# Alternate columns: a matmul that reads its moving operand from two halves in turn

## The chip, the cores and the metric

The kernel runs on one core of a Trainium2 chip. The time is device microseconds of one execution on that core; the kernel before takes 2062.57 us (median of three runs, 2061.97 to 2063.31). The core has TensorE (matmul), VectorE, ScalarE, GpSimd and SyncE; in the profile they are PE (and PEld for its loads of the stationary operand), DVE, ACT, POOL and SP. On-chip data stands in SBUF; TensorE writes its results to PSUM, from which VectorE and ScalarE read them ("evict" them).

## The reference

One inference step of a two-layer decoder trunk with 512 prompt tokens and 32 sample tokens (8 sequences of 4), in float32, model width 1024. Layer 0 mixes tokens with a gated MLP, layer 1 with attention over keys and values that layer 0's output produces once.

```python
for i in range(DEPTH):
    h = h + 0.5 * swiglu(rmsnorm(h, ffn1_norm[i]), ffn1_w1[i], ffn1_w3[i], ffn1_w2[i])
    xn = rmsnorm(h, mix_norm[i])
    if i < N_A:
        mix, v_rows = gmlp_mix(xn, gmlp_w_in[i], gmlp_v_norm[i], gmlp_w_s[i], gmlp_b_s[i], gmlp_w_out[i])
    else:
        q = rmsnorm((xn @ att_w_q[j]).reshape(bsz, L, N_HEADS, HEAD_DIM), q_norm[j])
        if past is None:
            o = fox_prompt(q, k, v, lf)
        else:
            o = fox_sample(q, k, v, lf, past[0], past[1], past[2])
        mix = o.reshape(bsz, L, D_ATT) @ att_w_o[j]
    h = h + mix
    h = h + 0.5 * swiglu(rmsnorm(h, ffn2_norm[i]), ffn2_w1[i], ffn2_w3[i], ffn2_w2[i])
    gate = jax.nn.sigmoid(rmsnorm(h, ple_norm[i]) @ ple_w_gate[i])
    h = h + gate * (pe[i] @ ple_w_proj[i])
    if i == N_A - 1:
        kv = shared_kv(h, kv_norm, w_kvf, b_f, k_norm)
```

`swiglu(x, w1, w3, w2)` is `(silu(x @ w1) * (x @ w3)) @ w2` with an inner width of 2816. Nearly all of the arithmetic lies in its four calls.

## The kernel before

The activations are kept transposed: 8 chunks of 128 features (partitions) by T = 544 token columns (512 of the prompt, 32 of the samples); HT = 272 is half of that. A float32 product is made of three: each operand is split into a high part, rounded to the type that the listing calls F32R, and a low part, and high·high, high·low and low·high are added up in PSUM. These are the **split products**. In a matmul the weights are the stationary operand (128 by 128), and the token columns are the moving one.

[...] `mm` (L229 on, matmuls at L241, L245 and L247) is the common form; `tile_mm` calls it with the next weights, and the caller evicts the result, always in one instruction on VectorE or ScalarE.

The first products of a feed-forward layer (`ffn_steps`) go by Strassen's scheme: `products` makes seven half-size products k = 1 to 7 in place of eight, each with 24 matmuls of 272 columns (L491), into the buffers A, B and C; `evict` copies or adds them together (L499 to L513). `second` makes the products by w2 through `mm`, and its `update` (L530) adds them to the residual stream. `ffn_slots` lays down in what order both kinds come; the four engines keep that order, since this part is scheduled by hand. Weights are loaded, split by ScalarE (L198) and VectorE (L199) and, for Strassen, added (L184) a few units ahead by `prepare`.

Other split products: the gated MLP, the gates, the keys and the queries by `tile_mm`; the last gate chunk by `cols_mm` (L675), which finishes one part of `COLS` before the other; the values by `v_group` (L829 to L831), where the weights are the moving operand, 256 columns wide; attention's output by `product` (L1268 to L1275). The products inside attention (L1107 to L1161, 256 to 512 columns) and the small transposes and sums are no part of the change.

Of the kernel before, what the change touches and what calls it, by code (L numbers as in the profile page):

```python
# [84 lines left out]

CUT = 256
COLS = ((0, CUT), (CUT, T))


def whole(p):  # L90

    return p[:].rearrange("p a b -> p (a b)")[:, 512 - CUT:512 - CUT + T]


class Builder:
# [133 lines left out]
    def mm(self, out, w, x, first, last, mid=None):  # L229

        nc = self.nc
        out = whole(out)
        n = len(w)
        pin, self.pins = self.pins > 0 and first, self.pins - first
        for k in range(n):
            (wh, wl), (xh, xl) = w[k], x[k]
            if mid is not None and k == n - 1:
                mid()
            s, e = first and k == 0, last and k == n - 1
            for a, b in COLS:  # L240
                i = nc.tensor.matmul(out[:, a:b], wh, xh[:, a:b], start=s, stop=False)  # L241
                if pin and k == 0:
                    self.tc.keep_in_program_order(i)
            for a, b in COLS:
                nc.tensor.matmul(out[:, a:b], wh, xl[:, a:b], start=False, stop=False)  # L245
            for a, b in COLS:
                nc.tensor.matmul(out[:, a:b], wl, xh[:, a:b], start=False, stop=e)  # L247

# [157 lines left out]
    def ffn(self, h, box, gcol, rstd, on_chunk, plain=1):  # L406

        nc, eng = self.nc, mybir.EngineType
        self.ahead = (2, 3, 6)
        first, xs, xf = [], self.pairs(box), box["f"]  # L410

        def more(n):
            if len(xf) < min(n, NKP):
                xf.append(self.forms(h, gcol, len(xf), xs))
        hid, todo = {}, ([], [])
        lead = plain == 1 and len(xf) < 3
        for f in range(2 * plain):
            g = self.big()
            for w in range(2):
                if lead:  # L420
                    more(len(xf) + 1)
                if rstd is None:
                    p, rstd = self.tile_rstd(xs, box["acc"])
                else:
                    p = self.tile_mm(xs)
                nc.scalar.copy(g[:, w], whole(p))
# [38 lines left out]
    def ffn_steps(self, h, xf, rstd, hid, todo, plain, on_chunk):  # L465
        nc = self.nc
        add = ALU.add
        tt = nc.vector.tensor_tensor
        q2 = lambda t: t.rearrange("p (w b) -> p w b", w=2)
        tail = len(PARTS) - 1  # L470
        after = []
        w_of, tiles = {}, {}

        def products(j, k, part):
# [11 lines left out]
            for kp in range(NKP):  # L486
                xh, xl = xf[kp][k]
                for n, (a, b) in enumerate(((hi, xh), (hi, xl), (lo, xh))):
                    for w in range(2):
                        c = slice(512 * w + P * kp, 512 * w + P * kp + P)  # L490
                        nc.tensor.matmul(dst[w], a[:, c], b, start=k in "152" and kp == 0 and n == 0,  # L491
                                         stop=kp == NKP - 1 and n == 2, skip_group_check=True)
            after.append(lambda: evict(j, k))

        def evict(j, k):
# [8 lines left out]
            if k == "2":  # L504
                for w in range(2):
                    tt(g[0][:, w, :HT], t["B"][w], t["r1"][:, w], add)
            elif k == "7":
                tt(g[1][:, :, HT:], t["A"], t["r5"], add)  # L508
            elif k == "3":
                tt(g[0][:, :, HT:], t["C"], t["r6"], add)  # L510
                todo[0].extend(self.gate(hid, rstd, j, 0, g[0]))
            else:
                nc.scalar.copy(g[1][:, :, :HT], t["A"])  # L513
                todo[1].extend(self.gate(hid, rstd, j, 1, g[1]))
                del tiles[j]

        def second(p, c, part):
# [11 lines left out]
            def update():  # L529
                nc.vector.scalar_tensor_tensor(h[c], whole(out), 0.5, h[c], ALU.mult, ALU.add)  # L530
                if p == tail:
# [38 lines left out]
    def gmlp(self, h, box, on_chunk):  # L570
# [17 lines left out]
        for c in range(NC_):  # L588
# [7 lines left out]
            def take(p=p, vc=vt[:, c % 2, :]):  # L596
                nc.vector.tensor_tensor(vc, whole(p), rstd, ALU.mult)
                self.ssq(sq, vc, first=not v)
# [5 lines left out]
        def u_tile(c):  # L604
# [3 lines left out]
            us[c] = us["t"][:, c % 2, :]  # L608
            nc.vector.tensor_tensor(us[c], whole(p), rstd, ALU.mult)

# [54 lines left out]
        for c in range(NC_):  # L665
            p = self.tile_mm(m)
            nc.vector.tensor_tensor(h[c], whole(p), h[c], ALU.add)
            on_chunk(c)

    def cols_mm(self, outs, w, x):  # L670

        for (a, b), out in zip(COLS, outs):
            for k, ((wh, wl), (xh, xl)) in enumerate(zip(w, x)):
                for n, (u, v) in enumerate(((wh, xh), (wh, xl), (wl, xh))):
                    i = self.nc.tensor.matmul(out[:, :b - a], u, v[:, a:b], start=k == 0 and n == 0,  # L675
                                              stop=k == len(w) - 1 and n == 2)
# [3 lines left out]
    def ple_last(self, h, gates, rstd, xs, wp, pp, y):  # L680
# [6 lines left out]
        for (u, v), out in zip(COLS, outs):  # L687
            tt(a[:, u:v], out[:, :v - u], rstd[:, u:v], ALU.mult)
            nc.scalar.activation(a[:, u:v], a[:, u:v], AF.Sigmoid)
        outs = [self.ps()[:, 0, :], self.ps()[:, 0, :]]  # L690
        self.cols_mm(outs, wp[2 * c:2 * c + 2], pp)
        for (u, v), out in zip(COLS, outs):
            tt(a[:, u:v], out[:, :v - u], a[:, u:v], ALU.mult)
            tt(h[c][:, u:v], h[c][:, u:v], a[:, u:v], ALU.add)
            nc.sync.dma_start(out=y[c][:, u:v], in_=h[c][:, u:v])

    def ple(self, h, box, layer, on_chunk):
# [11 lines left out]
        for c in range(NC_ + 2):  # L709
            if c < NC_:  # L710
# [5 lines left out]
                def gate(p1=p1):  # L716
                    a = self.tmp()
                    nc.vector.tensor_tensor(a, whole(p1), rstd, ALU.mult)
                    nc.scalar.activation(a, a, AF.Sigmoid)
# [5 lines left out]
            for n in (range(c - 2, c + 1) if last and c == NC_ - 2 else [c - 2] if c >= 2 else ()):  # L725
                p2 = self.ps()
                self.mm(p2, wp[2 * n:2 * n + 2], pp, True, True)
                a = gates[n]
                nc.vector.tensor_tensor(a, whole(p2), a, ALU.mult)
                nc.vector.tensor_tensor(h[n], h[n], a, ALU.add)  # L730
# [37 lines left out]
    def kv(self, h, box, ffn_gain):  # L768
# [4 lines left out]
        f = self.big()[:, 0, :]  # L773
        self.evac(lambda p=p: nc.vector.tensor_tensor(f, whole(p), rstd, ALU.mult))
        self.bg.append(self.forget(f))
# [11 lines left out]
        def k_tile(hh):  # L787
# [4 lines left out]
            def take(p=p, kc=box["k"][:, hh % 2, :]):  # L792
                box["last"] = nc.vector.tensor_tensor(kc, whole(p), rstd, ALU.mult)
                kraw.append(kc)
# [14 lines left out]
        def v_group(g, beside):  # L809
# [13 lines left out]
            for i in range(4):  # L823
# [3 lines left out]
                for k, (wh, wl) in enumerate(w):  # L827
                    xh, xl = xs[k]
                    nc.tensor.matmul(out, xh[:, t], wh, start=k == 0, stop=False)  # L829
                    nc.tensor.matmul(out, xh[:, t], wl, start=False, stop=False)  # L830
                    nc.tensor.matmul(out, xl[:, t], wh, start=False, stop=k == NC_ - 1)  # L831
                for f in beside[i]:
                    f()
            for i in range(4):
                nc.scalar.activation(vi[:, i], p[:, 256 * i:256 * i + 256].rearrange("p (h d) -> p h d", h=2), AF.Copy,
                                     scale=rc[:, i:i + 1])
# [196 lines left out]
    def queries(self, xs, acc):  # L1033
# [4 lines left out]
        def tile(h):  # L1038
# [7 lines left out]
            def take(p=p, qc=box["q"][:, h % 2, :]):  # L1046
                box["last"] = nc.vector.tensor_tensor(qc, whole(p), box["rstd"], ALU.mult)
                q[h], sqs[h] = qc, self.square(qc)
# [31 lines left out]
    def attention(self, xs, acc, h_out, on_chunk):  # L1080
# [181 lines left out]
        def product(out, hs, w, ks, late=False):  # L1262
            hi, lo = w
            pin, self.pins = self.pins > 0, 0
            for n, k in enumerate(ks):
                c = slice(P * n, P * n + P)
                s, e = n == 0, n == len(ks) - 1
                i = nc.tensor.matmul(out, hi[:, c], o[k][:, 0, hs], start=s, stop=False)  # L1268
                if pin and s:
                    self.tc.keep_in_program_order(i)  # L1270
                if not late:
                    nc.tensor.matmul(out, hi[:, c], o[k][:, 1, hs], start=False, stop=False)  # L1272
                nc.tensor.matmul(out, lo[:, c], o[k][:, 0, hs], start=False, stop=e and not late)  # L1273
            for n, k in enumerate(ks if late else ()):
                nc.tensor.matmul(out, hi[:, P * n:P * n + P], o[k][:, 1, hs], start=False, stop=n == len(ks) - 1)  # L1275

        def project_half(c, part):
# [8 lines left out]
            with self.tc.issue_after(behind.ins) if behind else nullcontext():  # L1286
                nc.vector.tensor_tensor(out, p[:, :, :HT], out, ALU.add)
            for a in range(2) if part == 1 else ():
                on_chunk(2 * c + a, slice(0, HT))

        def project(c):
# [4 lines left out]
            out = h_out[c][:, HT:]  # L1296
            nc.vector.tensor_tensor(out, p[:, 0, :HT], out, ALU.add)
            on_chunk(c, slice(HT, T))
# [230 lines left out]
```

## Time and profile before

| | before |
|---|---|
| median of three timed runs | 2062.57 us |
| profiled execution: span | 2060.8 us |
| instructions | 38,864 |
| HBM read, written | 218.95 MB, 16.49 MB |
| DMA, mean over the span | 115 GB/s |
| ScalarE, waiting for VectorE before L198 | 262.5 us |
| VectorE, waiting for TensorE before L530 | 106.4 us |
| ScalarE, waiting for TensorE before L499 | 141.3 us |

The profile was taken on one execution; it states its span, from the first to the last instruction, and no other time for that execution. Its page gives busy times and the chain of work that ended last. A row of a group reads: line, engine, operation, output<-input by the program's tile names, partitions x elements of one instruction, and the count; then busy time in us, the mean of one in ns, and the idle time of the engine just ahead of them with what ended it. A row of the timeline begins with its start and its duration in us; equal instructions in a row are merged and counted. The duration of a matmul covers its way through the pipeline, so neighbours overlap: what a matmul costs in a stream is the distance from one start to the next.

### The profile page before, as it was taken

How to read it: one execution, taken by the hardware profiler on the slowest of the kernel's cores; microseconds unless marked ns; L12 is line 12 of the kernel's file. 1: busy time of each engine (PE TensorE's matmuls, PEld its weight loads, DVE VectorE, ACT ScalarE, POOL GpSimd, SP SyncE). 2: the span in 40 equal slices, each digit the busy share in tenths (PEclk: the TensorE clock that was granted, in tenths of full speed). 3: DMA queues.
4: the chain of work that ended last, by engine and by line, in shares of the span. 5: the costliest groups of instructions: out<-in, count | busy, mean ns of one | idle time of the engine just before them, and what ended most of it. 6: DMA issues, size and time to landing. Idle time of an engine off the chain costs nothing.

```text
span 2060.8 us, 38864 instructions
## 1 busy us (share of the span) xinstructions
PE 2045.6 (99%) x16442; PEld 2013.9 (98%) x16442; DVE 1506.0 (73%) x1862; ACT 950.9 (46%) x1421; POOL 185.6 (9%) x222
## 2 busy tenths in 40 slices
PE   9999999999999999999999999999999999999999
PEld 8999999999999999999999999999987999999999
DVE  7877777556687778776688777776476888777774
ACT  7535344423554344454456343534364754344451
POOL 0000000410100000043060000001131200000020
PEclk9999999999999999999999999999999999999999
DMA  5233234312223232432374323324669232222421
GB/s 185 84 111 107 74 109 141 97 45 83 83 93 113 72 104 82 154 99 82 103 261 161 113 86 110 107 66 136 192 211 320 96 100 84 102 103 82 130 97 44
DMA packets 93823, 237.95 MB, mean 115 GB/s; under 512 B 9538, under 2 KB 27490, under 8 KB 93650
## 3 DMA queue, kind: packets, MB, share of 16 engines
q1 hardware_dynamic: 93506, 235.44, 34.3%
q8 instruction: 129, 2.11, 0.4%
q14 instruction: 44, 0.36, 0.0%
q10 hardware_dynamic: 144, 0.04, 0.0%
HBM read 218.95 MB, written 16.49 MB: 114 GB/s over the span
## 4 chain that ended last, share of the span: by engine, by line
PE 92%; DVE 3%; ACT 2%; issue 1%; DMA 1%; SPq 0%; POOL 0%; DVEq 0%; ACTq 0%; POOLq 0%
PE ps L491 33%; PE ps L241 16%; PE ps L247 16%; PE ps L245 15%; PE pb L491 5%; DVE big L199 1%; ACT big L198 1%; PE ps L1268 1%; PE ps L1273 1%; PE ps L1272 1%; DVE big L184 0%; PE ps L1223 0%; PE ps L829 0%; PE ps L830 0%; PE ps L831 0%
## 5 line engine op out<-in xcount | busy, mean ns | idle before, releaser
L491 PE MATMUL ps<-big,big 128*128 128x272 f32 x5616 | 727.6, 288 | 1.8 <-DVE big L508 1.3
L491 PEld LDWEIGHTS ps<-big,big 128*128 128x128 f32 x5616 | 714.2, 188 | 2.4 <-issue 1.6
L199 DVE TENSOR_TENSOR big<-big,big 128x1024 fp32r<-128x1024 f32 (+2 forms) x538 | 590.8, 1100 | 106.4 <-ACT big L198 106.0
L198 ACT CAST big<-big 128x1024 fp32r<-128x1024 f32 (+2 forms) x538 | 488.0, 932 | 267.8 <-DVE big L184 262.5
L241 PE MATMUL ps<-big,big 128*128 128x256 f32 (+1 forms) x2684 | 558.2, 289 | 1.2 <-ACT big L198 0.8
L247 PE MATMUL ps<-big,big 128*128 128x256 f32 x2684 | 554.0, 288 | 1.9 <-DVE big L199 1.9
L245 PE MATMUL ps<-big,big 128*128 128x256 f32 x2684 | 553.8, 287 | 0.1
L241 PEld LDWEIGHTS ps<-big,big 128*128 128x128 f32 x2684 | 429.8, 188 | 5.3 <-issue 1.7
L247 PEld LDWEIGHTS ps<-big,big 128*128 128x128 f32 x2684 | 429.3, 188 | 3.7 <-DVE big L199 3.2
L245 PEld LDWEIGHTS ps<-big,big 128*128 128x128 f32 x2684 | 432.3, 189 | 0.5 <-DVE big L298 0.5
L326 POOL TENSOR_TENSOR st<-st,tmp 128x544 f32<-128x544 f32 (+1 forms) x63 | 89.0, 1412 | 1587.0 <-ACT tmp L324 1586.8
L530 DVE SCALAR_TENSOR_TENSOR big<-ps,big 128x544 f32<-128x544 f32 x160 | 115.5, 722 | 106.6 <-PE ps L247 106.4
L184 DVE TENSOR_TENSOR big<-big,big 128x1024 f32<-128x1024 f32 x156 | 190.0, 1218 | 0.0
L499 ACT COPY tmp<-ps 128x544 f32<-128x544 f32 x117 | 71.9, 614 | 141.3 <-PE ps L491 141.3
L454 ACT ACTIVATE big<-big 128x544 f32<-128x544 f32 x88 | 58.0, 660 | 163.0 <-DVE big L451 161.8
L491 PE MATMUL pb<-big,big 128*128 128x272 f32 x936 | 124.0, 288 | 0.0
L451 DVE TENSOR_TENSOR big<-big,st 128x1088 f32<-128x1088 f32 x88 | 113.3, 1289 | 10.6 <-ACT big L513 8.9
L491 PEld LDWEIGHTS pb<-big,big 128*128 128x128 f32 x936 | 120.2, 188 | 0.0
L286 DVE TENSOR_TENSOR big<-big,big 128x544 fp32r<-128x544 f32 (+1 forms) x112 | 81.5, 734 | 36.7 <-ACT big L285 36.5
L297 ACT ACTIVATE big<-big,gains 128x544 fp32r<-128x544 f32 (+1 forms) x80 | 55.6, 704 | 105.9 <-DVE big L530 64.9
L298 DVE SCALAR_TENSOR_TENSOR big<-big,gains,big 128x544 fp32r<-128x544 f32 (+1 forms) x80 | 66.7, 843 | 25.2 <-ACT big L297 25.2
L285 ACT CAST big<-big 128x544 fp32r<-128x544 f32 (+1 forms) x112 | 71.3, 644 | 16.2 <-DVE big L457 8.9
(213 smaller groups left out, 1436.5 us busy)
## 6 DMA issues: line engine op xcount, KB each, us to landing
big<-in_w SPq DMA_DIRECT2D x156, 512.0 KB
big<-in_w2a SPq DMA_DIRECT2D x64, 512.0 KB
big<-in_w2b SPq DMA_DIRECT2D x32, 384.0 KB
big<-in_w13p SPq DMA_DIRECT2D x16, 512.0 KB
big<-in_win SPq DMA_DIRECT2D x16, 512.0 KB
big<-in_wg SPq DMA_DIRECT2D x16, 512.0 KB
big<-in_ck SPq DMA_DIRECT2D x16, 512.0 KB
big<-in_cv SPq DMA_DIRECT2D x16, 512.0 KB
```

The source lines that it names most:

```text
L184: self.nc.vector.tensor_tensor(t, a, b, ALU.add if op == "+" else ALU.subtract)
L198: self.nc.scalar.copy(hi, src)
L199: self.nc.vector.tensor_tensor(lo, src, hi.bitcast(F32), ALU.subtract)
L241: i = nc.tensor.matmul(out[:, a:b], wh, xh[:, a:b], start=s, stop=False)
L245: nc.tensor.matmul(out[:, a:b], wh, xl[:, a:b], start=False, stop=False)
L247: nc.tensor.matmul(out[:, a:b], wl, xh[:, a:b], start=False, stop=e)
L286: self.nc.vector.tensor_tensor(pair[:, 1, cols], src, pair[:, 0, cols].bitcast(F32), ALU.subtract)
L326: nc.gpsimd.tensor_tensor(acc[:, cols], acc[:, cols], sq, ALU.add)
L451: tt(g, g, rstd.unsqueeze(1).broadcast_to([P, 2, T]), ALU.mult)
L491: nc.tensor.matmul(dst[w], a[:, c], b, start=k in "152" and kp == 0 and n == 0, stop=kp == NKP - 1 and n == 2, skip_group_check=True)
L499: nc.scalar.copy(t["r" + k], t["C" if k == "5" else "A"])
L530: nc.vector.scalar_tensor_tensor(h[c], whole(out), 0.5, h[c], ALU.mult, ALU.add)
```

## The change

Five helpers rearrange the access patterns. `woven(x)` walks through a stretch of columns by taking one from its first half, one from its second, and so on; `turns(out)` gives the output the same shape without changing its order, so the results lie in PSUM in the order in which they were made. `unwoven` reads such a result with a step of two elements, first all columns of the first half and then all of the second; `halves` splits the other operands and the destination alike. Every matmul of the split products named above reads its moving operand through `woven`. `COLS` now cuts in the middle, at 272; in `mm` each of the two matmuls takes 136 columns of either half of the tile. In `products` the two streams are the halves of 272 columns, in `v_group` the halves of 256 weight columns, one head each.

```diff
-CUT = 256
-COLS = ((0, CUT), (CUT, T))
+COLS = ((0, HT), (HT, T))
+def woven(x):
+    return x.rearrange("p (a b) -> p b a", a=2)
+def turns(out):
+    return out.rearrange("p (b a) -> p b a", a=2)
+def unwoven(out):
+    return out.rearrange("p (b a) -> p a b", a=2)
+def halves(x):
+    return x.rearrange("p (a b) -> p a b", a=2)
+def span(p):
+    return p[:].rearrange("p a b -> p (a b)")[:, 512 - HT:512 - HT + T]
 def whole(p):
-    return p[:].rearrange("p a b -> p (a b)")[:, 512 - CUT:512 - CUT + T]
+    return unwoven(span(p))
...
     def mm(self, out, w, x, first, last, mid=None):
-        out = whole(out)
+        out = turns(span(out))
+        parts = [(out[:, a // 2:b // 2], slice(a // 2, b // 2)) for a, b in COLS]
...
-            (wh, wl), (xh, xl) = w[k], x[k]
+            (wh, wl), (xh, xl) = w[k], map(woven, x[k])
...
-            for a, b in COLS:
-                i = nc.tensor.matmul(out[:, a:b], wh, xh[:, a:b], start=s, stop=False)
+            for o, b in parts:
+                i = nc.tensor.matmul(o, wh, xh[:, b], start=s, stop=False)
...
-                        nc.tensor.matmul(dst[w], a[:, c], b, start=k in "152" and kp == 0 and n == 0,
+                        nc.tensor.matmul(turns(dst[w]), a[:, c], woven(b), start=k in "152" and kp == 0 and n == 0,
...
-                    tt(g[0][:, w, :HT], t["B"][w], t["r1"][:, w], add)
+                    tt(halves(g[0][:, w, :HT]), unwoven(t["B"][w]), unwoven(t["r1"][:, w]), add)
...
-                tt(g[1][:, :, HT:], t["A"], t["r5"], add)
+                tt(h4(g[1][:, :, HT:]), u4(t["A"]), u4(t["r5"]), add)
...
-                nc.vector.scalar_tensor_tensor(h[c], whole(out), 0.5, h[c], ALU.mult, ALU.add)
+                nc.vector.scalar_tensor_tensor(halves(h[c]), whole(out), 0.5, halves(h[c]), ALU.mult, ALU.add)
...
-                    nc.tensor.matmul(out, xh[:, t], wh, start=k == 0, stop=False)
+                    nc.tensor.matmul(turns(out), xh[:, t], woven(wh), start=k == 0, stop=False)
...
-                i = nc.tensor.matmul(out, hi[:, c], o[k][:, 0, hs], start=s, stop=False)
+                i = nc.tensor.matmul(turns(out), hi[:, c], woven(o[k][:, 0, hs]), start=s, stop=False)
```

The other evictions (the gated MLP, the gates, the keys, the queries, attention's output) are rewritten in the same way as the update of the feed-forward layer. No engine gets its instructions in another order. What differs in the rows is the cut, here on TensorE in the first product of the program (tile `ps_190`; `big_120` is the split input, `big_123` and `big_124` the parts of the weights). Before:

```order
L241 MATMUL ps_190<-big_120,big_123 128x256
L241 MATMUL ps_190<-big_120,big_123 128x288
L245 MATMUL ps_190<-big_120,big_123 128x256
L245 MATMUL ps_190<-big_120,big_123 128x288
L247 MATMUL ps_190<-big_120,big_124 128x256
L247 MATMUL ps_190<-big_120,big_124 128x288
```

and of the change, the same place and the six matmuls after it:

```order
L267 MATMUL ps_190<-big_120,big_123 128x272 x2
L271 MATMUL ps_190<-big_120,big_123 128x272 x2
L273 MATMUL ps_190<-big_120,big_124 128x272 x2
L267 MATMUL ps_190<-big_127,big_123 128x272 x2
L271 MATMUL ps_190<-big_127,big_123 128x272 x2
L273 MATMUL ps_190<-big_127,big_124 128x272 x2
```

The two matmuls of a pair now have the same width and stand merged in one row; nothing moved.

More of the change, by code (lines that the diff above doesn't have):

```diff
@@ L239, in mm @@
             s, e = first and k == 0, last and k == n - 1
-            for a, b in COLS:
-                i = nc.tensor.matmul(out[:, a:b], wh, xh[:, a:b], start=s, stop=False)
+            for o, b in parts:
+                i = nc.tensor.matmul(o, wh, xh[:, b], start=s, stop=False)
                 if pin and k == 0:
                     self.tc.keep_in_program_order(i)
[L244 to L247, printed above, removed]
+            for o, b in parts:
+                nc.tensor.matmul(o, wh, xl[:, b], start=False, stop=False)
+            for o, b in parts:
+                nc.tensor.matmul(o, wl, xh[:, b], start=False, stop=e)
     def tile_mm(self, xs, mid=None):
@@ L674, in cols_mm @@
                 for n, (u, v) in enumerate(((wh, xh), (wh, xl), (wl, xh))):
-                    i = self.nc.tensor.matmul(out[:, :b - a], u, v[:, a:b], start=k == 0 and n == 0,
+                    i = self.nc.tensor.matmul(turns(out[:, :b - a]), u, woven(v[:, a:b]), start=k == 0 and n == 0,
                                               stop=k == len(w) - 1 and n == 2)
@@ L1271, in product @@
                 if not late:
-                    nc.tensor.matmul(out, hi[:, c], o[k][:, 1, hs], start=False, stop=False)
-                nc.tensor.matmul(out, lo[:, c], o[k][:, 0, hs], start=False, stop=e and not late)
+                    nc.tensor.matmul(turns(out), hi[:, c], woven(o[k][:, 1, hs]), start=False, stop=False)
+                nc.tensor.matmul(turns(out), lo[:, c], woven(o[k][:, 0, hs]), start=False, stop=e and not late)
             for n, k in enumerate(ks if late else ()):
-                nc.tensor.matmul(out, hi[:, P * n:P * n + P], o[k][:, 1, hs], start=False, stop=n == len(ks) - 1)
+                nc.tensor.matmul(turns(out), hi[:, P * n:P * n + P], woven(o[k][:, 1, hs]), start=False,
+                                 stop=n == len(ks) - 1)
         def project_half(c, part):
@@ L1296, in project @@
             out = h_out[c][:, HT:]
-            nc.vector.tensor_tensor(out, p[:, 0, :HT], out, ALU.add)
+            nc.vector.tensor_tensor(halves(out), unwoven(p[:, 0, :HT]), halves(out), ALU.add)
             on_chunk(c, slice(HT, T))
```

37 lines of the change are left out of this document (20 added, 17 removed).

## The prediction

> **What bounds the kernel now.** I read the page first: busy time, clock, chain.
>
> ```profile
> span 2060.8 us, 38864 instructions
> ...
> PE 2045.6 (99%) x16442; PEld 2013.9 (98%) x16442; DVE 1506.0 (73%) x1862; ACT 950.9 (46%) x1421; POOL 185.6 (9%) x222
> ...
> PEclk9999999999999999999999999999999999999999
> ...
> PE 92%; DVE 3%; ACT 2%; issue 1%; DMA 1%; SPq 0%; POOL 0%; DVEq 0%; ACTq 0%; POOLq 0%
> PE ps L491 33%; PE ps L241 16%; PE ps L247 16%; PE ps L245 15%; PE pb L491 5%; DVE big L199 1%; ACT big L198 1%; PE ps L1268 1%; PE ps L1273 1%; PE ps L1272 1%; DVE big L184 0%; PE ps L1223 0%; PE ps L829 0%; PE ps L830 0%; PE ps L831 0%
> ```
>
> TensorE is the bound from end to end at full clock, and 85% of the chain are the matmuls of L491, L241, L245 and L247. A busy engine may still be slowed by something that feeds it, so the next question is how far apart two matmuls start. The timeline merges equal matmuls; a merged row of n lasts n−1 spacings plus one matmul of 288 ns.
>
> ```profile
> 643.36 6.18 PE L491 MATMUL ps<-big,big 128*128 128x272 f32 x48
> ...
> 652.37 9.23 PE L491 MATMUL ps<-big,big 128*128 128x272 f32 x72
> ...
> 664.46 0.41 PE L241 MATMUL ps<-big,big 128*128 128x256 f32 x2
> ...
> 667.20 0.41 PE L247 MATMUL ps<-big,big 128*128 128x256 f32 x2
> ```
>
> 272 columns: (6.18−0.29)/47 = 125.3 ns and (9.23−0.29)/71 = 125.9 ns; I use **125.6**. The last two rows are the first and the twelfth pair of one product (256 and 288 columns in each pair): (667.20−664.46)/11 = **249 ns** a pair.
>
> What would the array alone need? The trace has a stretch in which the clock was granted by half:
>
> ```profile
> 9.68 0.66 PE L247 MATMUL ps<-big,big 128*128 128x256 f32 x2
> 10.14 0.66 PE L241 MATMUL ps<-big,big 128*128 128x256 f32 x2
> 10.59 0.66 PE L245 MATMUL ps<-big,big 128*128 128x256 f32 x2
> 11.04 0.66 PE L247 MATMUL ps<-big,big 128*128 128x256 f32 x2
> ```
> ```profile
> 8.00:11.40 3.40, 3.02 (x12) 2.69 (x13) 3.18 (x5) 2.98 (x5) 0.00 (x0) 0.56 0.94 367
> ...
> 700.00:704.00 4.00, 4.00 (x35) 4.00 (x34) 3.06 (x5) 3.08 (x4) 0.00 (x0) 1.00 0.50 135
> ```
>
> (In the last two rows the third figure from the end is the granted clock, the last one GB/s.) At the low clock (0.56 over that window, whose end is already faster) a pair takes (11.04−9.68)/3 = 453 ns, 0.833 ns a column. Twice the clock should give 0.417 ns a column, 227 ns a pair and 113 ns for 272 columns. The full clock gives 249 and 125.6: **12 ns of each matmul are not array time**. Wider matmuls, which this change doesn't touch, tell how that splits:
>
> ```profile
> 1514.44 0.40 PE L1107 MATMUL ps<-big,big 128*128 128x512 f32 x1
> ...
> 1515.37 0.27 PE L1115 MATMUL ps<-neg,identr 128*128 128x256 f32 x1
> ```
> ```profile
> 1538.53 0.28 PE L1107 MATMUL ps<-big,big 128*128 128x256 f32 x1
> ...
> 1539.00 0.28 PE L1115 MATMUL ps<-neg,identr 128*128 128x256 f32 x1
> ...
> 1539.94 0.39 PE L1107 MATMUL ps<-big,big 128*128 128x512 f32 x1
> ...
> 1540.86 0.28 PE L1115 MATMUL ps<-neg,identr 128*128 128x256 f32 x1
> ```
>
> Between each row and the next shown stand four spacings: 232 and 230 ns at 512 columns, 117.5 ns at 256. The slope is (230 to 232−117.5)/256 = 0.44 to 0.45 ns a column, 0.023 to 0.033 over the array's 0.417. Of the 12 ns, **6 to 9 grow with the columns**; the rest is fixed. So at full clock something that hands columns over, not the array, sets the pace, by 6 to 8%. The change alters just the order in which columns are fetched.
>
> **The change part by part.** No instruction is added, removed or reordered on any engine; only the columns' order, the cut and the access patterns differ. How many matmuls it touches:
>
> ```profile
> L491 PE MATMUL ps<-big,big 128*128 128x272 f32 x5616 | 727.6, 288 | 1.8 <-DVE big L508 1.3
> ...
> L241 PE MATMUL ps<-big,big 128*128 128x256 f32 (+1 forms) x2684 | 558.2, 289 | 1.2 <-ACT big L198 0.8
> L247 PE MATMUL ps<-big,big 128*128 128x256 f32 x2684 | 554.0, 288 | 1.9 <-DVE big L199 1.9
> L245 PE MATMUL ps<-big,big 128*128 128x256 f32 x2684 | 553.8, 287 | 0.1
> ...
> L491 PE MATMUL pb<-big,big 128*128 128x272 f32 x936 | 124.0, 288 | 0.0
> ```
> ```profile
> L1268 PE MATMUL ps<-big,big 128*128 128x272 f32 x128 | 37.2, 292 | 0.3 <-ACT big L198 0.3
> L1273 PE MATMUL ps<-big,big 128*128 128x272 f32 x128 | 36.8, 289 | 0.5 <-DVE big L199 0.5
> L829 PE MATMUL ps<-big,big 128*128 128x256 f32 x128 | 36.5, 285 | 0.0
> L830 PE MATMUL ps<-big,big 128*128 128x256 f32 x128 | 36.2, 283 | 0.0
> L831 PE MATMUL ps<-big,big 128*128 128x256 f32 x128 | 36.1, 282 | 0.0
> L1272 PE MATMUL ps<-big,big 128*128 128x272 f32 x120 | 34.5, 288 | 0.0
> ```
>
> 5616+936+3·2684+2·128+3·128+120 = 15,364 of 16,442, all of them on the path.
>
> *Fetching alternately.* No row shows a matmul that reads so, so I bound it. Best: all 12 ns go, 15,364 × 12 = 184 us. Worst: two neighbouring columns never come from one place, and each costs what a column costs at the half clock, 0.833 ns: 272 × 0.833 + 3 = 230 ns, +104 ns each, +1,600 us. The ends are far apart. The nearest rows are the 256 and 512 column ones: they show a stall that grows with the run of neighbouring columns. If it belongs to moving on along such a run, two runs read in turn give each twice the time for that step, and the stall hides. I take 7 of the 6 to 9 ns: **−108 us**. This is a choice, not a measurement; the rivals take the other ends.
>
> [...] No run here shows a strided matmul yet.
>
> *The cut, 256/288 to 272/272* (4,026 pairs of L241 to L247): 2 × 125.6 − 249 = +2 ns a pair, **+8 us**. Bounds: nothing to +10, as the two 272 rows differ by 0.6 ns.
>
> *Evictions with a stride.*
>
> ```profile
> L530 DVE SCALAR_TENSOR_TENSOR big<-ps,big 128x544 f32<-128x544 f32 x160 | 115.5, 722 | 106.6 <-PE ps L247 106.4
> ...
> L506 DVE TENSOR_TENSOR big<-pb,tmp 128x272 f32<-128x272 f32 x78 | 30.6, 433 | 8.6 <-PE pb L491 8.6
> L508 DVE TENSOR_TENSOR big<-ps,tmp 128x544 f32<-128x544 f32 x39 | 28.2, 724 | 48.3 <-PE ps L491 48.3
> L510 DVE TENSOR_TENSOR big<-ps,tmp 128x544 f32<-128x544 f32 x39 | 28.2, 724 | 30.7 <-PE ps L491 30.5
> ```
> ```profile
> 650.00:1000.00 350.00, 350.00 (x2810) 349.97 (x2809) 259.87 (x292) 157.26 (x216) 39.69 (x32) 1.00 0.29 96
> ...
> 1520.00:1650.00 130.00, 126.63 (x1152) 112.24 (x1152) 97.04 (x184) 80.91 (x184) 34.18 (x69) 1.00 0.68 225
> ```
>
> A column more costs VectorE (724−433)/272 = 1.07 ns. Nothing shows a PSUM read with a stride, so the bounds are 0 and that again: +0.58 us for 544 columns, 238 × 0.58 + 78 × 0.29 = 161 us of VectorE work. VectorE is 260 of 350 us busy in a feed-forward layer (74%; the first row's sixth figure is its busy time), and the groups above were waiting for TensorE already. With 161 us more, VectorE would be at 1506 + 161 = 1667 of 2061 us, 81%. What is spare hides it, so I take 0; the cover is gone where TensorE waits for the eviction itself, and then each costs up to its 0.58 us.
>
> *What comes late next.* In attention (1520 to 1650) TensorE already waits 3.4 of 130 us; some of that stage's share of the gain is lost to those waits, +7 us. Weights arrive at 96 GB/s in the feed-forward window where another moved 367, so 5% more is covered. The load of the stationary operand, 98% busy on the page, must be asked too, since each matmul has one:
>
> ```profile
> 470.20 0.60 PE L618 MATMUL ps<-consts,big 128*128 128x128 f32 x4
> ```
>
> Four matmuls of 128 columns follow each other by (0.60−0.27)/3 = 110 ns (0.27 for one, next to the 0.28 of the 256-column rows), where their 128 columns need 53. So loads allow 110 ns, below the 118.6 that I forecast; they are no bound yet, and they would be one only past the best end.
>
> **Sum:** 2060.8 − 108 + 8 + 7 = 1967.8 us of span. The profile gives no time beyond the span; the timed median, 2062.57, lies 1.8 above it, so **about 1969 us**.
>
> [...]
>
> **Rivals.**
> 1. *Each column pays its own fetch* (slower). Place: all 15,364 matmuls. [...] Price: from zero to 0.417 ns a column; at the full price 2062.6+1600 ≈ 3660 us. It decides as soon as it costs more than the stall saves, 7 ns a matmul or 0.026 ns a column. A partial price of 0.07 ns a column would give about 2350. [...]
> 2. *The stall doesn't care about order*: it is a pause every so many columns, or the fixed part. Then only the cut remains: 2063 to 2071 us. For it: the same slope in 256 and 512 wide reads with different operands.
> 3. *Strided PSUM reads cost double and are not hidden* at the 160 updates of L530: if TensorE waits for every one, 160 × 0.58 = 93 us. Without a gain on TensorE 2062.6 + 8 + 93 = 2164; with it 2062. For it: L530 is the largest group that reads PSUM. Against: its 106.4 us of idle time before, spent waiting for TensorE.
>
> **How the numbers follow.** Forecast 0.48 (1900 to 2055 by its own bounds). Rival 1: 0.30, of it 0.12 with a partial price (2067 to 2350), 0.18 beyond. Rival 2: 0.16, of it 0.10 within 0.2% (about what a measurement here can tell from no change). Rival 3: 0.06, of it 0.02 still faster. So faster 0.50, same 0.10, slower 0.40. Leaving out rival 1's expensive part (0.18) and 0.02 of tails, the range is 1900 to 2350; the likeliest case alone would be 1900 to 2055.
>
> **What would show it.** Right: runs of 24 to 72 matmuls of the Strassen line at 117 to 120 ns instead of 125.6, TensorE still at 98% or more, VectorE's evictions still at 722 ns. Rival 1: spacings well over 126, up to 230 ns, with every other engine waiting. Rival 2: 125.6 unchanged. Rival 3: L530's mean near 1,300 ns instead of 722 and TensorE waiting for it. The forecast fails first at its choice of 7 ns, since no row of this trace prices an alternate read.

## The result

The changed kernel takes 1936.35 us (median of four runs, 1936.06 to 1937.12) against 2062.27 us for the kernel before: a ratio of 0.939, 95% interval 0.9377 to 0.9404. 126 us are gone. The page of the profiled execution after:

```profile
span 1934.7 us, 38865 instructions
...
PE 1908.8 (99%) x16442; PEld 1873.7 (97%) x16442; DVE 1502.2 (78%) x1862; ACT 946.9 (49%) x1421; POOL 185.3 (10%) x222
...
PE 85%; DVE 7%; ACT 4%; issue 2%; DMA 2%; SPq 1%; POOL 0%; DVEq 0%; ACTq 0%
```

The same number of matmuls in 136.8 us less of busy time (2045.6 to 1908.8), and all other engines as busy as before, to within 4 us. TensorE is still 99% busy: that figure said nothing of the room that was there. The time in which TensorE isn't busy (span less its busy time) went from 15.2 (2060.8 − 2045.6) to 25.9 us (1934.7 − 1908.8); 136.8 − 10.7 = 126.1 us is the gain in span.

The timeline of TensorE after (start, duration, instruction, count) has the spacings:

```profile
603.33 5.72 PE L519 MATMUL ps<-big,big 128*128 128x272 f32 x48
608.89 0.40 PE L267 MATMUL ps<-big,big 128*128 128x272 f32 x2
...
611.44 0.40 PE L273 MATMUL ps<-big,big 128*128 128x272 f32 x2
611.67 8.50 PE L519 MATMUL ps<-big,big 128*128 128x272 f32 x72
```

272 columns: (5.72−0.28)/47 and (8.50−0.28)/71 give **115.8 ns** both times (0.28 us is the last matmul alone), where the rows before gave 125.3 and 125.9. A pair of the common form takes (611.44−608.89)/11 = 231.8 ns instead of 249. The evictions, in the groups by shape (the last row is ScalarE's largest; before, at L499, its mean was 614 ns):

```profile
L558 DVE SCALAR_TENSOR_TENSOR big<-ps,big 128x544 f32<-128x544 f32 x160 | 115.4, 721 | 75.8 <-PE ps L273 75.8
...
L534 DVE TENSOR_TENSOR big<-pb,tmp 128x272 f32<-128x272 f32 x78 | 30.7, 437 | 1.8
L536 DVE TENSOR_TENSOR big<-ps,tmp 128x544 f32<-128x544 f32 x39 | 28.2, 724 | 35.7 <-PE ps L519 35.7
L538 DVE TENSOR_TENSOR big<-ps,tmp 128x544 f32<-128x544 f32 x39 | 28.1, 722 | 25.9 <-PE ps L519 25.9
```
```profile
L527 ACT COPY tmp<-ps 128x544 f32<-128x544 f32 x117 | 71.5, 611 | 89.7 <-PE ps L519 89.7
```

721, 437, 724 and 722 ns against 722, 433, 724 and 724 on VectorE, 611 against 614 on ScalarE: reading PSUM in steps of two float32 costs neither engine anything that these rows can show, beyond the 4 ns of the 272-wide row. What did shrink is their idle time, since TensorE comes round sooner: 75.8 us before L558 where it was 106.6.

### The profile page after: what moved, and what is told of

Read it like the earlier page. It is cut to its first block, busy times and chain, and to the rows that moved or that the text cites. A ratio compares the mean times of both kernels' runs of the same rounds, so it can differ in the third digit from the quotient of the medians.

```text
span 1934.7 us, 38865 instructions
## 1 busy us (share of the span) xinstructions
PE 1908.8 (99%) x16442; PEld 1873.7 (97%) x16442; DVE 1502.2 (78%) x1862; ACT 946.9 (49%) x1421; POOL 185.3 (10%) x222
## 4 chain that ended last, share of the span: by engine, by line
PE 85%; DVE 7%; ACT 4%; issue 2%; DMA 2%; SPq 1%; POOL 0%; DVEq 0%; ACTq 0%
PE ps L519 30%; PE ps L267 14%; PE ps L273 14%; PE ps L271 14%; PE pb L519 5%; DVE big L224 2%; ACT big L223 1%; DVE big L209 1%; DVE big L312 1%; DMA tmp<-rows 1%; ACT big L311 1%; DVE big L477 0%; PE ps L1251 0%; PE ps L657 0%; PE ps L857 0%
## 5 line engine op out<-in xcount | busy, mean ns | idle before, releaser
L519 PE MATMUL ps<-big,big 128*128 128x272 f32 x5616 | 674.1, 279 | 5.9 <-DVE big L536 3.4
L519 PEld LDWEIGHTS ps<-big,big 128*128 128x128 f32 x5616 | 660.8, 189 | 7.1 <-issue 4.0
L224 DVE TENSOR_TENSOR big<-big,big 128x1024 fp32r<-128x1024 f32 (+2 forms) x538 | 593.7, 1106 | 88.7 <-ACT big L223 87.2
L223 ACT CAST big<-big 128x1024 fp32r<-128x1024 f32 (+2 forms) x538 | 485.1, 928 | 271.1 <-DVE big L209 267.1
L267 PE MATMUL ps<-big,big 128*128 128x272 f32 x2684 | 533.5, 280 | 5.6 <-ACT big L223 4.0
L273 PE MATMUL ps<-big,big 128*128 128x272 f32 x2684 | 531.5, 279 | 3.6 <-DVE big L224 3.5
L271 PE MATMUL ps<-big,big 128*128 128x272 f32 x2684 | 530.6, 279 | 0.3 <-DVE big L324 0.3
L267 PEld LDWEIGHTS ps<-big,big 128*128 128x128 f32 x2684 | 409.6, 189 | 11.5 <-ACT big L223 7.3
L273 PEld LDWEIGHTS ps<-big,big 128*128 128x128 f32 x2684 | 409.2, 189 | 6.1 <-DVE big L224 5.7
L271 PEld LDWEIGHTS ps<-big,big 128*128 128x128 f32 x2684 | 409.4, 189 | 0.8 <-DVE big L324 0.7
L558 DVE SCALAR_TENSOR_TENSOR big<-ps,big 128x544 f32<-128x544 f32 x160 | 115.4, 721 | 75.8 <-PE ps L273 75.8
L519 PE MATMUL pb<-big,big 128*128 128x272 f32 x936 | 114.8, 279 | 0.0
L519 PEld LDWEIGHTS pb<-big,big 128*128 128x128 f32 x936 | 111.3, 189 | 0.0
```

The costliest lines, as they stand in the source:

```text
L223: self.nc.scalar.copy(hi, src)
L224: self.nc.vector.tensor_tensor(lo, src, hi.bitcast(F32), ALU.subtract)
L267: i = nc.tensor.matmul(o, wh, xh[:, b], start=s, stop=False)
L271: nc.tensor.matmul(o, wh, xl[:, b], start=False, stop=False)
L273: nc.tensor.matmul(o, wl, xh[:, b], start=False, stop=e)
L519: nc.tensor.matmul(turns(dst[w]), a[:, c], woven(b), start=k in "152" and kp == 0 and n == 0, stop=kp == NKP - 1 and n == 2, skip_group_ch ...
```

## The experiments

Three sorts: streams of matmuls put ahead of the changed kernel's work, which price one way of reading each; the change done or undone in part; and one version that goes further. A stream is 24 matmuls with one operand each; its spacing is (duration of its row − the last matmul's duration) / 23, and the text gives the mean over its start times. The kernel's own work follows unchanged, so the total times of those runs mean nothing here.

### Streams, first set (bench)

```diff
+        x, w, hx = self.flat(1024, F32R), self.flat(1024, F32R), self.flat(1024, mybir.dt.bfloat16)
...
+        weave = lambda n, a=2: x[:, :n].rearrange("p (a b) -> p b a", a=a)
+        group = lambda n, c: x[:, :n].rearrange("p (a b c) -> p b a c", a=2, c=c)
+        local = lambda n, b: x[:, :n].rearrange("p (g a b) -> p g b a", a=2, b=b)
+        step = lambda n, a: x[:, :n].rearrange("p (b a) -> p a b", a=a)
...
+        for _ in R: mm(o(272), W, x[:, :272], start=True, stop=True)
+        for _ in R: mm(f3(272, 2), W, weave(272), start=True, stop=True)
...
```

Here `mm` is the matmul, `R` the 24 repetitions, `W` 128 columns of weights, and `o` and `f3` shape the output. `step` reads every a-th column, then goes back for the next set, until all are read. `local` takes turns between neighbouring runs of b columns, `group` takes c columns at a time from each half. Each set was profiled in one execution. Where a row stands in two sets, the two agree within 1.4 ns: contiguous 272 columns took 125.3 and 126.7 ns, woven ones 115.9 and 116.0, two columns at a time 175.4 and 174.6.

> The changed kernel with 31 streams of 24 matmuls each put ahead of its work, on one float32 operand (F32R) of random numbers, 128 by 128 weights; a stream's spacing is read from its row of the timeline. Theory A (the stall belongs to moving on along one run of neighbouring columns, and two runs read in turn hide it): contiguous 256, 272, 384, 512 columns at about 117, 125, 176, 232 ns; woven halves at N x 0.417 + 2.5 = 109 to 112, 116, 162.5, 216 ns; four and eight streams as two, 116; pairs and fours of neighbours read in turn lie between 116 and 125; two streams only 2 or 4 columns apart still share one run and stay at 122 to 125, those 16 or 64 columns apart reach 109 to 112 at 256 columns. [...] Theory C (the stall is a conflict with the load of the next weights): loading 32 instead of 128 weight columns takes it away from contiguous reading too, 116 ns; and a single column read 272 times over still has it. Theory D (it is the width of the element): two-byte operands have no stall when contiguous, 116 ns at 272 and 216 ns at 512 columns, and the weave changes nothing for them.

The rows of the timeline, in order: contiguous and woven at 272, 256, 384 and 512 columns (L1356 to L1363); then four and eight streams (L1364, L1365); further down two streams 2 and 4 columns apart (L1370, L1371), steps of 2 and 4 (L1375, L1376), 32 columns of weights, contiguous (L1382), and two-byte columns, contiguous (L1384, 272 wide) and woven (L1386, 512 wide).

```profile
14.60 3.17 PE L1356 MATMUL pb<-big,big 128*128 128x272 f32 x24
17.61 2.94 PE L1357 MATMUL pb<-big,big 128*128 128x272 f32 x24
20.39 3.03 PE L1358 MATMUL pb<-big,big 128*128 128x256 f32 x24
23.25 2.84 PE L1359 MATMUL pb<-big,big 128*128 128x256 f32 x24
25.93 4.36 PE L1360 MATMUL pb<-big,big 128*128 128x384 f32 x24
30.14 4.06 PE L1361 MATMUL pb<-big,big 128*128 128x384 f32 x24
34.03 5.65 PE L1362 MATMUL pb<-big,big 128*128 128x512 f32 x24
39.52 5.34 PE L1363 MATMUL pb<-big,big 128*128 128x512 f32 x24
44.70 3.65 PE L1364 MATMUL pb<-big,big 128*128 128x272 f32 x24
48.19 5.77 PE L1365 MATMUL pb<-big,big 128*128 128x272 f32 x24
...
67.12 3.18 PE L1370 MATMUL pb<-big,big 128*128 128x272 f32 x24
70.14 2.94 PE L1371 MATMUL pb<-big,big 128*128 128x272 f32 x24
...
81.06 6.08 PE L1375 MATMUL pb<-big,big 128*128 128x272 f32 x24
86.96 6.10 PE L1376 MATMUL pb<-big,big 128*128 128x272 f32 x24
...
112.68 3.20 PE L1382 MATMUL pb<-big,big 128*32 128x272 f32 x24
...
118.50 2.95 PE L1384 MATMUL pb<-big 128*128 128x272 bf16 x24
...
126.47 11.79 PE L1386 MATMUL pb<-big 128*128 128x512 bf16 x24
```

| read | ns | read | ns |
|---|---|---|---|
| contiguous 256, 272, 384, 512 | 119.4, 125.3, 175.1, 228.8 | woven halves, same widths | 111.7, 115.9, 162.4, 215.8 |
| two streams 2, 4, 8 columns apart (272) | 125.9, 115.8, 115.8 | two streams 16, 64 apart (256) | 111.6, 111.7 |
| four, eight streams (272) | 145.2, 232.7 | 2, 4, 8 columns at a time (272) | 175.4, 131.0, 130.0 |
| step 2, 4, 8 (272); step 16 (256) | 246.1, 246.6, 233.4; 219.8 | one column for ever (272) | 119.9 |
| contiguous, starting 1 or 2 columns later (272) | 125.3, 126.5 | 16 columns at a time (256) | 120.0 |
| weights of 32 columns: contiguous, woven (272) | 126.5, 115.7 | two-byte: contiguous 272, 512; woven 512 | 116.3, 215.9; 484.3 |

The 2.5 ns that theory A adds to N x 0.417 is what the changed kernel's 115.8 ns leave over 272 columns at the half-clock estimate of 0.417 (113.3). Theory C falls: with 32 columns of weights to load in place of 128 the stall stays (126.5), and a woven read with the same weights has none (115.7). D holds for its first half, two-byte columns don't stall when contiguous (116.3 ns at 272, 215.9 at 512); weaving them costs more than double (484 against 216), which nobody expected. A is right about two halves (115.9), but not about runs: 4 columns apart, inside one run, is as good as half a tile apart (115.8), while 2 apart is worth nothing (125.9), and four streams are worse than one (145.2 against 125.3). Four float32 are 16 bytes, and columns 2 apart still share 16 bytes where columns 4 apart don't: the rows fit a memory that is read in lines of 16 bytes. This is inferred from spacings, and "line" means no more than that from here on. Steps are dear, as rival 1 had it (246.1, 246.6 and 233.4 ns at steps of 2, 4 and 8), but step 2 visits each line twice in a row and still pays the double (246.1), while the weave leaves a line after every column and pays nothing (115.9). So neither the number of visits in a row nor the distance decides. A new theory was needed. E and F, which follow, both build on this line; the two hits that E asks of a line fit contiguous reading, where a line holds two even and two odd columns of the stream (125.3 ns), against step 2, where it holds one of each (246.1).

### The cut alone (cut_alone), and the weave with the old cut (weave_256)

`COLS` says where the 544 columns of a product are cut for its two matmuls: 256 and 288 columns in the kernel before.

```diff
-CUT = 256
+CUT = HT
```

> The kernel before with the cut moved from 256 to 272 and nothing else. The prediction's term: +8 us, 2071 us, the pairs of the common form at 251 ns instead of 249. If the cut is free: 2062 us within 2.

```profile
PE 2052.9 (99%) x16442; PEld 2021.4 (98%) x16442; DVE 1507.4 (73%) x1862; ACT 950.9 (46%) x1421; POOL 186.7 (9%) x222
```

2069.35 us, ratio 1.0034 (1.0021 to 1.0046): **+6.6 us**, where the prediction had +8. TensorE's busy time is 2052.9 us, 7.3 more than before. The cut by itself made the kernel slower, by 0.3%; all of the gain is from the order of reading. In the second run the changed kernel gets the old cut:

```diff
-COLS = ((0, HT), (HT, T))
+CUT = 256
+COLS = ((0, CUT), (CUT, T))
...
-    return p[:].rearrange("p a b -> p (a b)")[:, 512 - HT:512 - HT + T]
+    return p[:].rearrange("p a b -> p (a b)")[:, 512 - CUT:512 - CUT + T]
```

> The changed kernel with the cut back at 256 and 288 columns, still read alternately. If the woven spacing is N x 0.417 + 2.5 ns whatever N is: the pairs take 109.2 + 122.5 = 231.7 ns as at 272 and 272, 1936 us within 2. If 256 columns meet the floor that the loads of the stationary operand set (112 ns for the value products, which are 256 wide): about +2.5 ns for each of 4,026 pairs, 1946 us.

1946.02 us (1945.24 to 1947.21), the second case. The stream rows above show the floor: 256 woven columns take 111.7 ns, not 109.2, and 128 columns before took 110; the value products of the changed kernel, 256 columns wide, start 111 to 112 ns apart (L857 to L859). A load of 128 stationary columns goes with each of these matmuls (on the page PE and PEld both count 16,442). That this load sets the floor is an inference, borne out by two rows of the changed kernel, both at a granted clock of 1.00:

```profile
922.28 0.95 PE L830 MATMUL pb<-consts,st 128*128 128x1 f32 x8
...
1438.08 1.32 PE L1212 MATMUL pb<-big,big 128*32 128x128 f32 x40
```

In the first, each matmul has a single moving column; from the second on they still start 111 to 112 ns apart. In the second, the matmuls load 32 columns each and go four together: 40 of them take 1.32 us, and from the second group of four on the groups start 109 to 113 ns apart, some 27 ns for a matmul, so a matmul as such isn't bound to 110 ns. No stream of 256 woven columns with fewer stationary columns was run, which would settle it. At 272 columns the array (113.3 ns by the half-clock estimate) has passed that floor. Woven, the equal cut is the better one by 10 us; contiguous, it was the worse one by 7.

### Streams, second set (bench2)

> Seventeen more streams of 24 matmuls ahead of the changed kernel's work. Theory E (the columns of even and of odd number in a stream have a reader each, which keeps the last 16-byte line it fetched; a line serves it at full speed when it is hit at least twice, and the two get into each other's way now and then when they want the same line): two woven streams that each step by 2 columns hit a line twice per reader, without sharing, and run at 112 to 120 ns for 256 columns; stepping by 4 they hit it once, 213 to 235 ns; each column read twice over has both readers on one line, 117 to 125 ns at 272 columns; starts 2 columns late or halves 138 apart make no difference, 116 ns; sixteen streams as eight, about 220 ns. Theory F (there are two line buffers for all columns, and what counts is how many lines are fetched): two streams that step by 2 fetch as many lines as one stream that steps by 2, which took 246 ns at 272 columns, so about 230 ns at 256; each column twice fetches half as many as contiguous, 116 ns. For two-byte columns both theories expect that taking two neighbours (4 bytes) from each half in turn brings 512 columns from 484 back to 216 ns, if the reader works in 4-byte words, and no change at 484 ns, if it pairs columns only within one contiguous run.

The timeline's rows for two woven streams that each step by 2 (L1361) and by 4 (L1362) at 256 columns, and for each column twice over at 272 (L1364):

```profile
20.27 3.04 PE L1361 MATMUL pb<-big,big 128*128 128x256 f32 x24
23.15 5.61 PE L1362 MATMUL pb<-big,big 128*128 128x256 f32 x24
...
32.67 2.95 PE L1364 MATMUL pb<-big,big 128*128 128x272 f32 x24
```

120.0 ns, 226.0 ns and 116.2 ns. Theory F, which counts the lines fetched, had about 230 for the first, so it falls; E had 112 to 120 and 213 to 235. But E's own reason for the stall of a contiguous read, that two readers want the same line, falls too: each column twice over puts both on the same column all the time and runs at 116.2, and the streams of L1361 share no line and stall like contiguous ones (119.4). What is left of E is the count of hits that each reader gets from one line. Halves that start two columns late or lie 138 apart ran at 115.9 and 115.8, as expected. Sixteen streams took 219.5, as expected, six 153.1, four 143.8, and four that each step by 2 took 170.6. Two-byte columns, 512 wide: 2 at a time 271.5, 4 at a time 226.9, 8 at a time 215.7, and a single step of 2 took 225.9. That is neither of the two expectations (2 at a time was to bring either 216 or no change at 484); of the turns that ran, of 1, 2, 4 and 8 columns, only those of 8, 16 bytes from one place, took what contiguous columns take (215.7 against 215.9).

### Streams, third set (bench3)

> Eleven more streams, 272 columns each. Theory G (a reader for the even and one for the odd columns of a stream; a 16-byte line that serves its reader four times in a row costs nothing, twice 8%, once the double): each column read twice over while stepping by 2 hits a line twice per reader, 125 ns; stepping by 4 once, 230 ns; each column four times over hits a line eight, four and two times per reader when stepping by 1, 2 and 4: 116, 116 and 125 ns; two columns of two lines in turn for ever, 116 ns. Theory F (what counts is the number of lines that the stream fetches, whoever reads them): twice over by 2 fetches 68 lines as the contiguous read does, 125 ns, twice over by 4 fetches 136 and four times over by 4 fetches 68, 246 and 125 ns; one more sign would be the plain steps of the first run, where 2 and 4 columns fetch 136 and 272 lines and yet both took 246. A single column for ever: 116 ns by both theories, whatever its place; the first run had 120, so if it is 120 again at other places, something else than fetching stands in that row.

The rows for each column twice over, stepping by 2 and 4 (L1359, L1360), and four times over, stepping by 1, 2 and 4 (L1361 to L1363):

```profile
20.44 3.20 PE L1359 MATMUL pb<-big,big 128*128 128x272 f32 x24
23.47 6.00 PE L1360 MATMUL pb<-big,big 128*128 128x272 f32 x24
29.28 2.98 PE L1361 MATMUL pb<-big,big 128*128 128x272 f32 x24
32.09 2.94 PE L1362 MATMUL pb<-big,big 128*128 128x272 f32 x24
34.87 3.17 PE L1363 MATMUL pb<-big,big 128*128 128x272 f32 x24
```

126.6, 242.0, 117.3, 115.8 and 125.4 ns. Theory G had 125, 230, 116, 116 and 125: all five go its way, the second 12 ns above. F has them too in these rows (246 for the second, which is nearer), so this run doesn't part the two; the steps of the first set and L1361 of the second do. Two columns of two lines in turn for ever took 117.7, where G had 116. A single column took 118.5 to 118.6 at three places, where both theories had 116; that stays open.

### Only the Strassen products as before (strassen_contiguous)

```diff
-                        nc.tensor.matmul(turns(dst[w]), a[:, c], woven(b), start=k in "152" and kp == 0 and n == 0,
+                        nc.tensor.matmul(dst[w], a[:, c], b, start=k in "152" and kp == 0 and n == 0,
...
-                tt(h4(g[1][:, :, HT:]), u4(t["A"]), u4(t["r5"]), add)
+                tt(g[1][:, :, HT:], t["A"], t["r5"], add)
...
```

> The changed kernel with the Strassen products and their evictions as before; all other split products stay woven. If the gain is 9.8 ns for each matmul on the path, 6,552 of them cost 64 us: 1936 + 64 = 2000 us. If part of the gain in the Strassen stages had been eaten by evictions or waits, less than 64 us comes back: 1960 to 1990 us.

```profile
PE 1970.3 (99%) x16442; PEld 1936.1 (97%) x16442; DVE 1504.0 (76%) x1862; ACT 949.6 (48%) x1421; POOL 185.4 (9%) x222
```

1993.88 us (1993.53 to 1994.81), 57.5 us more than the changed kernel: between the two expectations. TensorE's busy time rises by 61.5 us (1908.8 to 1970.3), that is 9.4 ns for each of the 6,552; and the time in which it isn't busy falls from 25.9 to 21.5 us (1991.8 − 1970.3). So the price for each matmul is the same here as in the streams (9.4), and 4.4 us of these 61.5 had turned into waits.

### Attention's own products woven too (weave_attention, weave_attention2, after_again)

```diff
+def bwoven(x):
+    return x.rearrange("p (g a b) -> p g b a", a=2, b=64)
...
+                to = bturns(out[:, :w])
...
+                nc.tensor.matmul(to, qp[:, 0, qs], bwoven(kp[:, 0, :w]), start=False, stop=False)
...
-                nc.scalar.activation(p[:, :w], sc, AF.Exp, bias=m, accum_out=l)
+                nc.scalar.activation(bhalves(p[:, :w]), bunwoven(sc), AF.Exp, bias=m, accum_out=l)
```

> The changed kernel with the products inside attention woven too, in halves of each block of 128 columns, and read back with a stride by the softmax's exponential and the split of attention's output. 256 matmuls of 256, 384 and 512 columns lose 7.7, 12.7 and 13 ns each: 2.5 us in all. If TensorE is the bound in that stage: 1933.8 us. If the softmax's and the splits' chains are: no change, 1936 us within 1.

1934.45 us (1933.44 to 1935.64). The difference to 1936.35 is 1.9 us, and the kernel before has medians from 2062.27 to 2063.49 us in the rounds of these experiments, so both kernels ran again in the same rounds.

> The changed kernel as it is, on the same chip and in the same rounds as the next run, for comparison: 1936 us within 1.

> The products inside attention woven too, as in the run of that name before. If TensorE's 2.2 us of work less count in that stage: 2.2 us below the changed kernel of these rounds. If the softmax's chains hide them: within 0.5 us of it.

1936.72 us (1935.94 to 1938.17) and **1934.45 us** (1934.26 to 1935.56): 2.3 us less, the first case, and no run of the one overlaps the other. Against the kernel before the ratios are 0.9388 (0.9375 to 0.9401) and 0.9378 (0.9365 to 0.9390). TensorE's busy time is 1906.6 us in the profile of weave_attention, against 1908.8 in the changed kernel's. This version is the fastest of all that ran, by 0.1%.

## Why the prediction held, step by step

The direction, the mechanism's place (the fetching of the moving columns, on TensorE) and the range were right, and the gain was larger than forecast: 126 us against 93. The reason why the order of reading should matter was right only in part. The prediction gave "faster" no more than even chances and its range reached to 2350 us, so the direction was in part luck. Term by term:

| term | predicted | measured |
|---|---|---|
| fetching alternately | −108 us (7 ns x 15,364) | −144 us (1908.8 − 2052.9 of busy time), 9.4 ns |
| the cut | +8 | +7 (2052.9 − 2045.6) |
| strided evictions | 0 | 0 (721 ns against 722) |
| waits that come late next | +7 | +11 (25.9 − 15.2) |
| span | −93 | −126 |

**The half-clock argument** (12 ns of each matmul aren't array time, so something that feeds the array holds it up) was the step that showed the room; that the order of reading would win it was a choice. Woven, 113.3 of 115.8 ns are array time by the same estimate. One reading beside it is wrong and does no harm: it is the start of the window from 8.00 to 11.40 us, not its end, that had a higher clock (0.72 from 8 to 9 us); in the four rows used, from 9.68 to 11.04 us, the granted clock was 0.50.

**The mis-sized term** is the choice of 7 ns. It rested on splitting the 12 ns by the slope between 256 and 512 columns into 6 to 9 that grow with the columns and a fixed rest. The streams show that split to be wrong: contiguous and woven reads differ by 7.7, 9.4, 12.7 and 13.0 ns at 256, 272, 384 and 512 columns (the first is held back by the floor of 111.7). The stall grows with the width, but less than in proportion, and nearly all of it goes when two halves take turns: over the array's time (0.417 ns a column, the half-clock estimate) 2.4 to 2.6 ns stay at 272 columns and more. The spacing of 115.8 lies even below the 117 to 120 that were to show the forecast right.

**Why a stall hides** was put as two runs that give each other twice the time for moving on. As a reason this failed: two streams 4 columns apart in one run (115.8), or one run with each column read twice (116.2), lose the stall as well, and four runs, which would give each other more time still, cost 145.2 instead of 125.3. Two was the right number of runs without the reason for it. Theory G, a reader for each, says it more closely: what counts is how often one 16-byte line serves the even columns of the stream, and how often the odd ones. It fits every row of float32 in which one or two streams are read a column at a time, but for the single column that stays 3 ns above it: four hits by the same reader cost nothing (at 272 columns weave 115.9 ns, 4 columns apart 115.8, each column twice 116.2), two hits cost some 8% (contiguous 125.3, 2 apart 125.9, twice with step 2 126.6; weave with step 2 120.0 at 256 columns, where the plain weave took 111.7), one hit costs the double (steps of 2 to 8 246.1, 246.6 and 233.4, twice with step 4 242.0; weave with step 4 226.0 at 256 columns). It is inferred from spacings; nothing in a trace shows such readers. And a reader that holds one line doesn't explain the other rows: four streams and two columns at a time give each reader one hit in a row, so they should cost the double, and take 145 and 175 ns; eight at a time is two hits, 125 ns by the theory, and takes 130. Nor does it hold for two-byte columns, where the weave gives each reader eight hits in a row and takes 484 ns. How it is built stays open.

**Rival 1** (each column pays its own fetch) was given 0.30 and the worst end; no run had priced an alternate read by then. Its price is real, but not for this order: steps of 2 or 4 columns, and eight streams, run at 233 to 247 ns, which is the forecast's 230 for the double price. Had the change read from eight places in turn instead of two, that rival would have come true (232.7). Nor is it leaving a line that costs: step 2 hits each line twice in a row and takes 246 ns, the weave once and takes 115.9.

**Rival 2** (the stall doesn't care about order) falls with the 115.8, **rival 3** (evictions at double price) with the 721. The prediction priced VectorE's strided evictions alone and left out ScalarE's, without a reason; they cost nothing either (611 ns against 614 at the largest group).

**The waits** came in the forecast's size, but mostly not at its place. TensorE's own waits, before and then after:

```profile
PE ps L247 <- DVE big L199: 1.9, 4, 0.5
...
PE ps L491 <- DVE big L508: 1.3, 2, 0.7
...
PE ps L241 <- ACT big L198: 0.8, 2, 0.5
...
PE ps L491 <- ACT tmp L499: 0.5, 1, 0.5
```
```profile
PE ps L267 <- ACT big L223: 4.0, 6, 1.4
PE ps L273 <- DVE big L224: 3.5, 8, 0.6
PE ps L519 <- DVE big L536: 3.4, 3, 2.1
PE ps L519 <- ACT tmp L527: 2.5, 3, 1.3
```

(Who waited for whom: us in total, times, longest.) The splits of the weights (L198 and L199, now L223 and L224) and the Strassen evictions took 4.5 us of waits in these rows and now take 13.4. The prediction looked for them in attention, where the products' waits for the softmax stayed at 1.6 and 0.5 us; they came in the Strassen stages and before products whose weights had only just been split. That the sum came near the forecast's +7 is luck.

## What to carry to other kernels

An engine that is 99% busy may still spend 8% of each instruction on its operands (here 9.4 of 125.3 ns): compare the distance between starts with what a half-clock stretch, or another width, says of the array alone. For four-byte moving operands, let neighbouring columns of a matmul come from two places in turn, four columns (16 bytes) apart or more (115.8 ns for 272 columns against 125.3 contiguous and 125.9 at 2 apart), write the results in that order, and undo it in the eviction, which cost VectorE (721 ns against 722) and ScalarE (611 against 614) nothing here; take exactly two streams (four took 145.2), and don't do it with two-byte operands (484.3 ns for 512 columns against 215.9). When the spacing falls, look again at the cut: here 256 woven columns met a floor of 112 ns, by all signs the load of the stationary operand, and 272 took 115.9, of which the array alone takes 113.3 by the half-clock estimate.

## What the runs showed of the hardware that was not expected

- A contiguous read of float32 columns was not the fastest: 125.3 ns for 272 against 115.9 in two turns.
- Four streams (145 ns for 272 columns) were slower than one (125), eight cost nearly the double (233).
- Stepping by 2 columns cost as much as stepping by 4: 246.1 and 246.6 ns for 272.
- Two-byte columns read in turns of one cost 484 ns for 512 columns instead of 216, more than twice; in turns of eight (16 bytes) 216 again (215.7).
- Reads of PSUM in steps of 8 bytes cost what contiguous ones did, on VectorE (721 and 722 ns for 544 columns) and on ScalarE (611 and 614).
- Rows of matmuls that each load 128 stationary columns stayed at some 110 ns a matmul with few moving columns too: 110 ns with 128 (L618 before), 112 with a single one (L830 after).
